# Row sums of a 67 MB array: blocks of 32 rows with a store each, a body on VectorE alone, and a two-piece last row

## The chip, the cores and the metric

The kernel runs on one core of a Trainium2 chip. The metric is the time of an execution on the device in microseconds (us), as a median of several executions. The granted clock was 1.00 in every profiled run.

A profiled "span" is about 1.8 us shorter than the timed execution, because it leaves out part of start and end.

## The reference

```python
def setup_inputs():
    batch, seq, dim = 32, 512, 1024
    return {"x": np.random.randn(batch, seq, dim).astype(np.float32)}

def reference(x):
    return np.sum(x, axis=-1).astype(np.float32)
```

There are 16384 rows of 1024 floats, 67.1 MB in, and 64 KB out. Each of the 128 partitions sums 128 rows.

## The kernel before

A partition owns 128 consecutive rows, so neighbouring partitions lie 128 x 4 KB = 512 KB apart in HBM. A full tile holds 16 rows a partition (8.39 MB). Three buffers rotate. VectorE sums one half of the tile in one instruction and ScalarE the other half row by row. The last tile is loaded in falling sizes, so that little is left to add when the last bytes arrive.

```python
    x_p = x_flat.rearrange("(p c) d -> p (c d)", p=P)      # C = 128 rows a partition
    out2d = out.rearrange("a (b c) -> (a b) c", c=C)
    G = 16
    T = C // G
    xpool = ctx.enter_context(tc.tile_pool(name="x", bufs=3))
    res = rpool.tile([P, C], F32, name="res")
    ...
    for t in range(T - 1):
        c0 = t * G
        xt = xpool.tile([P, G * D], F32, tag="xt", name="xt")
        load(xt, c0, 0, G * D)
        rows_dve(xt, c0, 0, G // 2)            # one tensor_reduce over 8 rows
        rows_act(xt, c0, G // 2, G // 2)       # 8 activations with accum_out

    c0 = (T - 1) * G                           # the last tile: 8, 4, 2, 1 rows, then
    ...                                        # the last row in 512 + 256 + 256 columns
    for j, n in runs:
        if n > 1:
            rows_dve(xt, c0, j, n // 2)
            rows_act(xt, c0, j + n // 2, n // 2)
        else:
            rows_act(xt, c0, j, 1)
    acc = [part[:, 0:1], part[:, 1:2], res[:, C - 1 : C]]
    for i, (a, b) in enumerate(zip(cuts, cuts[1:])):
        pairs_dve(xt, a, b, acc[i - 1] if i else 0.0, acc[i])   # half + half, summed

    nc.sync.dma_start(out=out2d, in_=res)      # 512 B a partition
```

Of the kernel before, what the change touches and what calls it, by code (L numbers as in the profile page):

```python
# [1 line left out]

# [4 lines left out]

F32 = mybir.dt.float32
ADD = mybir.AluOpType.add


@with_exitstack
def kernel(
    ctx: ExitStack,
    tc: tile.TileContext,
    x: bass.AP,
    out: bass.AP,
):
    nc = tc.nc
    P = nc.NUM_PARTITIONS  # L20

    x_flat = x.flatten_outer_dims()
    R, D = x_flat.shape
    assert R % P == 0
    C = R // P

    x_p = x_flat.rearrange("(p c) d -> p (c d)", p=P)
    out2d = out.rearrange("a (b c) -> (a b) c", c=C)

    G = 16  # L30
    assert C % G == 0
    T = C // G

    xpool = ctx.enter_context(tc.tile_pool(name="x", bufs=3))
    rpool = ctx.enter_context(tc.tile_pool(name="res", bufs=1))
    res = rpool.tile([P, C], F32, name="res")
    part = rpool.tile([P, 4], F32, name="part")

    def load(xt, c0, a, b):
        nc.sync.dma_start(out=xt[:, a:b], in_=x_p[:, c0 * D + a : c0 * D + b])  # L40

    def rows_dve(xt, c0, j, n):
        nc.vector.tensor_reduce(  # L43
            out=res[:, c0 + j : c0 + j + n],
            in_=xt[:, j * D : (j + n) * D].rearrange("p (j d) -> p j d", d=D),
            axis=mybir.AxisListType.X,
            op=ADD,
        )

    def rows_act(xt, c0, j, n):  # L50
        for i in range(j, j + n):
            v = xt[:, i * D : (i + 1) * D]
            nc.scalar.activation(  # L53
                out=v,
                in_=v,
                func=mybir.ActivationFunctionType.Copy,
                accum_out=res[:, c0 + i : c0 + i + 1],
            )

    def pairs_dve(xt, a, b, first, acc):  # L60
        h = (b - a) // 2
        nc.vector.tensor_tensor_reduce(  # L62
            out=xt[:, a : a + h],
            in0=xt[:, a : a + h],
            in1=xt[:, a + h : b],
            scale=1.0,
            scalar=first,
            op0=ADD,
            op1=ADD,
            accum_out=acc,  # L70
        )

    for t in range(T - 1):
        c0 = t * G
        xt = xpool.tile([P, G * D], F32, tag="xt", name="xt")
        load(xt, c0, 0, G * D)
        rows_dve(xt, c0, 0, G // 2)
        rows_act(xt, c0, G // 2, G // 2)

    c0 = (T - 1) * G  # L80
    xt = xpool.tile([P, G * D], F32, tag="xt", name="xt")
    j = 0
    runs = []
    for n in (8, 4, 2, 1):
        load(xt, c0, j * D, (j + n) * D)
        runs.append((j, n))
        j += n
    cuts = [j * D + k for k in (0, D // 2, 3 * D // 4, D)]
    for a, b in zip(cuts, cuts[1:]):
        load(xt, c0, a, b)  # L90

    for j, n in runs:
        if n > 1:
            rows_dve(xt, c0, j, n // 2)
            rows_act(xt, c0, j + n // 2, n // 2)
        else:
            rows_act(xt, c0, j, 1)
    acc = [part[:, 0:1], part[:, 1:2], res[:, C - 1 : C]]
    for i, (a, b) in enumerate(zip(cuts, cuts[1:])):
        pairs_dve(xt, a, b, acc[i - 1] if i else 0.0, acc[i])  # L100

    nc.sync.dma_start(out=out2d, in_=res)


# [1 line left out]
_INS = ['x']  # L106
_OUTS = [((32, 512), 'float32')]


# [23 lines left out]
```

## Time and profile before

| | before |
|---|---|
| median of 3 runs | 163.96 us (163.91 to 163.97) |
| span of the profiled run (164.13 us) | 162.4 us |
| DMA engines busy (page, part 3) | 96.3% |
| VectorE, ScalarE busy (page, part 1) | 43%, 43% |
| interval of full tiles | 19.4 us for 8.39 MB |
| last load landed; last VectorE instruction ended | 159.12; 159.86 us |

The first lines are from the page of the kernel before: busy time of the engines, the DMA queues with the share of time in which the 16 DMA engines were busy, and the shares of the chain that ended last.

```profile
DVE 69.9 (43%) x16; ACT 69.0 (43%) x129; POOL 0.2 (0%) x4
...
q1 hardware_dynamic: 2160, 67.18, 96.3%
...
DMA 85%; DVE 11%; SPq 1%; issue 1%; DVEq 0%
```

Next is the timeline of VectorE in the kernel before. The columns are start, duration (both us), engine, line, operation and shapes. The bracket gives the idle time before the instruction and what ended it. CUSTOM_DVE_ANT_0 is the instruction that adds two halves and sums the result (`pairs_dve`); DVE_READ_ACCUMULATOR2_ANT then writes its sum out.

```profile
22.97 8.69 DVE L43 TENSOR_REDUCE res<-xt 128x8 f32<-128x8192 f32 x1 [22.97 <-DMA xt<-in_x_dram]
42.27 8.69 DVE L43 TENSOR_REDUCE res<-xt 128x8 f32<-128x8192 f32 x1 [10.62 <-DMA xt<-in_x_dram]
61.96 8.69 DVE L43 TENSOR_REDUCE res<-xt 128x8 f32<-128x8192 f32 x1 [11.00 <-DMA xt<-in_x_dram]
...
139.44 8.69 DVE L43 TENSOR_REDUCE res<-xt 128x8 f32<-128x8192 f32 x1 [10.66 <-DMA xt<-in_x_dram]
149.16 4.42 DVE L43 TENSOR_REDUCE res<-xt 128x4 f32<-128x4096 f32 x1 [1.04 <-DMA xt<-in_x_dram]
...
158.64 0.42 DVE L62 CUSTOM_DVE_ANT_0 xt<-xt 128x256 f32<-128x256 f32 x1 [0.87 <-DMA xt<-in_x_dram]
158.99 0.08 DVE L62 DVE_READ_ACCUMULATOR2_ANT part<- 128x1 f32 x1
159.11 0.35 DVE L62 CUSTOM_DVE_ANT_0 xt<-xt,part 128x128 f32<-128x128 f32 x1
159.38 0.08 DVE L62 DVE_READ_ACCUMULATOR2_ANT part<- 128x1 f32 x1
159.50 0.35 DVE L62 CUSTOM_DVE_ANT_0 xt<-xt,part 128x128 f32<-128x128 f32 x1
159.78 0.08 DVE L62 DVE_READ_ACCUMULATOR2_ANT res<- 128x1 f32 x1
```

VectorE waits for a load before every full tile, so the load stream sets the pace. Tiles come 19.3 to 19.7 us apart, about 432 GB/s. The Trainium skill, "DMA: Bandwidth & Descriptors" (Specifications), puts the fabric ceiling at 435 GB/s, and this trace agrees. So in a kernel like this the time is made of three parts: when the stream gets going, 67.1 MB at a fixed rate, and what follows the last byte.

The first tile is there only at 22.97 us, although its load was issued at 0.73 us and a tile takes 19.4.

### The profile page before, as it was taken

To read this page: it belongs to the slowest core of one execution; us is meant where nothing else is said; L and a number is where in the kernel's file an instruction comes from. 1 tells how busy PE (TensorE), PEld (TensorE's weight loads), DVE (VectorE), ACT (ScalarE), POOL (GpSimd) and SP (SyncE) were. 2 spreads that over 40 slices of the span, in tenths; PEclk is the share of its full clock that TensorE was granted. 3 is DMA by queue.
4 is the path that set the end of the run, shared out by engine and by line. 5 is a ranking of instruction groups with operands and counts; after the bars stand their busy time and mean duration, and the time that the engine had idled before them with its cause. 6 is when DMAs were issued, how large, how long until landed. Compare 5 with 4: busy or idle time off the path is not lost.

```text
span 162.4 us, 220 instructions
## 1 busy us (share of the span) xinstructions
DVE 69.9 (43%) x16; ACT 69.0 (43%) x129; POOL 0.2 (0%) x4
## 2 busy tenths in 40 slices
DVE  0000039700595007940099101990049700697882
ACT  3000039700594007930099101990039600696881
POOL 0000000000000000000000000000000000000000
DMA  7979989989989989989997997997997997999980
GB/s 258 517 323 452 517 355 420 517 371 404 501 355 436 517 371 404 517 371 404 517 452 325 517 468 307 517 468 323 501 484 323 484 484 307 452 420 408 418 350 20
DMA packets 2161, 67.18 MB, mean 414 GB/s; under 512 B 240, under 2 KB 624, under 8 KB 880
## 3 DMA queue, kind: packets, MB, share of 16 engines
q1 hardware_dynamic: 2160, 67.18, 96.3%
q14 instruction: 1, 0.01, 0.0%
HBM read 67.11 MB, written 0.07 MB: 414 GB/s over the span
## 4 chain that ended last, share of the span: by engine, by line
DMA 85%; DVE 11%; SPq 1%; issue 1%; DVEq 0%
DMA xt<-in_x_dram 85%; DVE res L43 11%; SPq L40 1%; DVE xt L62 0%; DVE part L62 0%; DVEq L62 0%; DVEq L128 0%
## 5 line engine op out<-in xcount | busy, mean ns | idle before, releaser
L43 DVE TENSOR_REDUCE res<-xt 128x8 f32<-128x8192 f32 (+3 forms) x10 | 68.7, 6873 | 89.0 <-DMA xt<-in_x_dram 89.0
L53 ACT ACTIVATE xt<-xt 128x1024 f32<-128x1024 f32 x64 | 66.7, 1043 | 89.3 <-DMA xt<-in_x_dram 89.1
L53 ACT ACTIVATION_READ_ACCUMULATOR xt<-xt 128x1 f32 x64 | 11.9, 187 | 0.0
L53 ACT ACT_TABLE_LOAD x1 | 1.3, 1283 | 0.7 <-PEq L117 0.7
L62 DVE CUSTOM_DVE_ANT_0 xt<-xt 128x256 f32<-128x256 f32 x1 | 0.4, 425 | 0.9 <-DMA xt<-in_x_dram 0.9
L62 DVE CUSTOM_DVE_ANT_0 xt<-xt,part 128x128 f32<-128x128 f32 x2 | 0.7, 352 | 0.1
L62 DVE DVE_READ_ACCUMULATOR2_ANT part<- 128x1 f32 x2 | 0.2, 82 | 0.0
L117 POOL MEMSET const-bfloat16-1.0<- 128x1 bf16 x1 | 0.1, 101 | 0.0
L117 POOL MEMSET const-uint8-127<- 128x1 uint8 x1 | 0.1, 101 | 0.0
L117 POOL MEMSET const-float32-0.0<- 128x1 f32 x1 | 0.1, 98 | 0.2 <-issue 0.2
L117 POOL MEMSET const-float32-1.0<- 128x1 f32 x1 | 0.1, 98 | 0.0
L62 DVE DVE_READ_ACCUMULATOR2_ANT res<- 128x1 f32 x1 | 0.1, 84 | 0.0
## 6 DMA issues: line engine op xcount, KB each, us to landing
xt<-in_x_dram SPq DMA_DIRECT2D x1, 4096.0 KB, 39.7
xt<-in_x_dram SPq DMA_DIRECT2D x1, 2048.0 KB, 44.2
xt<-in_x_dram SPq DMA_DIRECT2D x1, 1024.0 KB, 46.2
xt<-in_x_dram SPq DMA_DIRECT2D x1, 512.0 KB, 47.0
xt<-in_x_dram SPq DMA_DIRECT2D x1, 256.0 KB, 47.1
xt<-in_x_dram SPq DMA_DIRECT2D x2, 128.0 KB, 43.0
xt<-in_x_dram SPq DMA_DIRECT2D x7, 49.4
out_dram<-res SPq DMA_DIRECT2D x1, 64.0 KB, 1.5
```

The source lines that it names most:

```text
L40: nc.sync.dma_start(out=xt[:, a:b], in_=x_p[:, c0 * D + a : c0 * D + b])
L43: nc.vector.tensor_reduce(out=res[:, c0 + j : c0 + j + n], in_=xt[:, j * D : (j + n) * D].rearrange("p (j d) -> p j d", d=D), axis=mybir.A ...
L53: nc.scalar.activation(out=v, in_=v, func=mybir.ActivationFunctionType.Copy, accum_out=res[:, c0 + i : c0 + i + 1],)
L62: nc.vector.tensor_tensor_reduce(out=xt[:, a : a + h], in0=xt[:, a : a + h], in1=xt[:, a + h : b], scale=1.0, scalar=first, op0=ADD, op1=A ...
L117: nc = _bacc.Bacc("TRN2", target_bir_lowering=False, num_devices=1)
```

## The change

The intent is to shorten what follows the last byte. The rows are split into four blocks of 4096. Within a block a partition owns 32 consecutive rows, so partitions lie 32 x 4 KB = 128 KB apart. Each block has its own result tile and its own store; three of the four stores go out during the stream, and the last one has 128 B a partition instead of 512 B. VectorE alone sums the body, so that ScalarE is free. ScalarE joins for 6 rows of the last full tile and for the tail. The last row comes in two pieces (640 and 384 columns) instead of three. The first piece is shared by both engines, and a last reduce adds 384 columns and the two partial sums.

The diff is shortened: `...` marks what is left out, and long calls stand on one line.

```diff
+BLOCKS = (32, 32, 32, 32)
...
+ACT_ROWS = 6
+CUT = 640
...
+    def block(r0, n):
+        x_b = x_flat[r0 : r0 + P * n].rearrange("(p c) d -> p (c d)", p=P)
+        out_b = out_flat[r0 : r0 + P * n].rearrange("(p c) -> p c", p=P)
+        return x_b, out_b, rpool.tile([P, n], F32, name=f"res{r0}")
...
-    for t in range(T - 1):
...
-        load(xt, c0, 0, G * D)
-        rows_dve(xt, c0, 0, G // 2)
-        rows_act(xt, c0, G // 2, G // 2)
...
+    for b, n in enumerate(BLOCKS):
+        x_b, out_b, res = block(r0, n)
...
+            nc.sync.dma_start(out=xt[:, 0 : m * D], in_=x_b[:, c * D : (c + m) * D])
+            a = ACT_ROWS if final and c + m == whole else 0
+            rows_dve(xt, res, 0, m - a, c)
+            rows_act(xt, res, m - a, a, c + m - a)
+            c += m
+        if not final:
+            nc.scalar.dma_start(out=out_b, in_=res)
...
-    for i, (a, b) in enumerate(zip(cuts, cuts[1:])):
-        pairs_dve(xt, a, b, acc[i - 1] if i else 0.0, acc[i])
-    nc.sync.dma_start(out=out2d, in_=res)
+    row_pairs_dve(xt, res, i + 2, c + i + 2)          # the last row but one
+    nc.vector.tensor_reduce(out=tail[:, D : D + 1], in_=tail[:, 0 : CUT // 2], axis=X, op=ADD)
+    sum_act(tail[:, CUT // 2 : CUT], tail[:, D + 1 : D + 2])
+    nc.vector.tensor_reduce(out=res[:, n - 1 : n], in_=tail[:, CUT : D + 2], axis=X, op=ADD)
+    nc.sync.dma_start(out=out_b, in_=res)
```

More of the change, by code (lines that the diff above doesn't have):

```diff
@@ L9 @@
 ADD = mybir.AluOpType.add
+COPY = mybir.ActivationFunctionType.Copy
+X = mybir.AxisListType.X
+BLOCKS = (32, 32, 32, 32)
+G = 16
+ACT_ROWS = 6
+CUT = 640
 @with_exitstack
@@ L23 @@
     R, D = x_flat.shape
-    assert R % P == 0
     C = R // P
-    x_p = x_flat.rearrange("(p c) d -> p (c d)", p=P)
-    out2d = out.rearrange("a (b c) -> (a b) c", c=C)
-    G = 16
-    assert C % G == 0
-    T = C // G
+    assert R % P == 0 and sum(BLOCKS) == C
+    out_flat = out.rearrange("a (b c) -> (a b c)", c=1)
     xpool = ctx.enter_context(tc.tile_pool(name="x", bufs=3))
     rpool = ctx.enter_context(tc.tile_pool(name="res", bufs=1))
-    res = rpool.tile([P, C], F32, name="res")
@@ L37, with rows_dve @@
-    part = rpool.tile([P, 4], F32, name="part")
-    def load(xt, c0, a, b):
-        nc.sync.dma_start(out=xt[:, a:b], in_=x_p[:, c0 * D + a : c0 * D + b])
-    def rows_dve(xt, c0, j, n):
+    tail = rpool.tile([P, D + 2], F32, name="tail")
+    def rows_dve(xt, res, j, n, c):
         nc.vector.tensor_reduce(
-            out=res[:, c0 + j : c0 + j + n],
+            out=res[:, c : c + n],
             in_=xt[:, j * D : (j + n) * D].rearrange("p (j d) -> p j d", d=D),
-            axis=mybir.AxisListType.X,
+            axis=X,
@@ L47, in rows_dve @@
             op=ADD,
         )
-    def rows_act(xt, c0, j, n):
-        for i in range(j, j + n):
-            v = xt[:, i * D : (i + 1) * D]
-            nc.scalar.activation(
-                out=v,
-                in_=v,
-                func=mybir.ActivationFunctionType.Copy,
-                accum_out=res[:, c0 + i : c0 + i + 1],
-            )
-    def pairs_dve(xt, a, b, first, acc):
-        h = (b - a) // 2
-        nc.vector.tensor_tensor_reduce(
-            out=xt[:, a : a + h],
-            in0=xt[:, a : a + h],
-            in1=xt[:, a + h : b],
-            scale=1.0,
-            scalar=first,
-            op0=ADD,
-            op1=ADD,
-            accum_out=acc,
-        )
@@ L73 @@
-    for t in range(T - 1):
-        c0 = t * G
-        xt = xpool.tile([P, G * D], F32, tag="xt", name="xt")
-        load(xt, c0, 0, G * D)
-        rows_dve(xt, c0, 0, G // 2)
-        rows_act(xt, c0, G // 2, G // 2)
-    c0 = (T - 1) * G
-    xt = xpool.tile([P, G * D], F32, tag="xt", name="xt")
-    j = 0
-    runs = []
-    for n in (8, 4, 2, 1):
-        load(xt, c0, j * D, (j + n) * D)
-        runs.append((j, n))
-        j += n
-    cuts = [j * D + k for k in (0, D // 2, 3 * D // 4, D)]
@@ L89, with sum_act @@
-    for a, b in zip(cuts, cuts[1:]):
-        load(xt, c0, a, b)
-    for j, n in runs:
-        if n > 1:
-            rows_dve(xt, c0, j, n // 2)
-            rows_act(xt, c0, j + n // 2, n // 2)
-        else:
-            rows_act(xt, c0, j, 1)
-    acc = [part[:, 0:1], part[:, 1:2], res[:, C - 1 : C]]
-    for i, (a, b) in enumerate(zip(cuts, cuts[1:])):
-        pairs_dve(xt, a, b, acc[i - 1] if i else 0.0, acc[i])
-    nc.sync.dma_start(out=out2d, in_=res)
+    def sum_act(v, acc):
+        nc.scalar.activation(out=v, in_=v, func=COPY, accum_out=acc)
@@ new lines, in rows_act, with row_pairs_dve @@
+    def rows_act(xt, res, j, n, c):
+        for i in range(n):
+            sum_act(xt[:, (j + i) * D : (j + i + 1) * D], res[:, c + i : c + i + 1])
+    def row_pairs_dve(xt, res, j, c):
+        h = D // 2
+        a, b = xt[:, j * D : j * D + h], xt[:, j * D + h : (j + 1) * D]
+        nc.vector.tensor_tensor_reduce(
+            out=a, in0=a, in1=b, scale=1.0, scalar=0.0, op0=ADD, op1=ADD,
+            accum_out=res[:, c : c + 1],
+        )
+    def block(r0, n):
+        x_b = x_flat[r0 : r0 + P * n].rearrange("(p c) d -> p (c d)", p=P)
+        out_b = out_flat[r0 : r0 + P * n].rearrange("(p c) -> p c", p=P)
+        return x_b, out_b, rpool.tile([P, n], F32, name=f"res{r0}")
@@ new lines @@
+    r0 = 0
+    for b, n in enumerate(BLOCKS):
+        x_b, out_b, res = block(r0, n)
+        r0 += P * n
+        final = b == len(BLOCKS) - 1
+        whole = n - G - (n % G if final and n % G else 0) if final else n
+        c = 0
+        while c < whole:
+            m = min(G, whole - c)
+            xt = xpool.tile([P, G * D], F32, tag="xt", name="xt")
+            nc.sync.dma_start(out=xt[:, 0 : m * D], in_=x_b[:, c * D : (c + m) * D])
[5 more added lines that the diff above has]
+            nc.scalar.dma_start(out=out_b, in_=res)
@@ new lines @@
+    xt = xpool.tile([P, G * D], F32, tag="xt", name="xt")
+    first = n - c - 8
+    cuts = [0, first, first + 4, first + 6, first + 7]
+    for i, k in zip(cuts, cuts[1:]):
+        nc.sync.dma_start(out=xt[:, i * D : k * D], in_=x_b[:, (c + i) * D : (c + k) * D])
+    last = (n - 1) * D
+    nc.sync.dma_start(out=tail[:, 0:CUT], in_=x_b[:, last : last + CUT])
+    nc.sync.dma_start(out=tail[:, CUT:D], in_=x_b[:, last + CUT : last + D])
+    for i, k in zip(cuts[:2], cuts[1:3]):
+        h = (k - i + 1) // 2
+        rows_dve(xt, res, i, h, c + i)
+        rows_act(xt, res, i + h, k - i - h, c + i + h)
@@ L106 @@
+    i = cuts[2]
+    rows_dve(xt, res, i, 1, c + i)
+    rows_act(xt, res, i + 1, 1, c + i + 1)
+    row_pairs_dve(xt, res, i + 2, c + i + 2)
+    nc.vector.tensor_reduce(
+        out=tail[:, D : D + 1], in_=tail[:, 0 : CUT // 2], axis=X, op=ADD
+    )
+    sum_act(tail[:, CUT // 2 : CUT], tail[:, D + 1 : D + 2])
+    nc.vector.tensor_reduce(
+        out=res[:, n - 1 : n], in_=tail[:, CUT : D + 2], axis=X, op=ADD
+    )
+    nc.sync.dma_start(out=out_b, in_=res)
 _INS = ['x']
```

## The prediction

> **What bounds the kernel now.** The DMA engines: busy 96.3% of the 162.4 us span on the page; VectorE and ScalarE 43% each. The chain of waits gives DMA 85%, VectorE 11%. In the timeline the reduces of full tiles start at 42.27, 61.96, 81.33, 100.73, 120.09 and 139.44 us: 19.4 us per 8.39 MB tile, about 432 GB/s. The Trainium skill ("DMA: Bandwidth & Descriptors", Specifications) puts the fabric ceiling at 435 GB/s; this trace agrees, so the body has nothing to gain. A 64 KB packet takes 2.42 us. Only about 2 us of start and the tail remain: the last load lands near 159.1 us, VectorE ends at 159.86, the store lands about 1.5 us after issue.
>
> **What the change does.**
> 1. Body: VectorE alone sums 16 rows. From the groups by form, 8 rows take 8.69 us and 4 take 4.42: 1.067 us a row and 0.15 fixed, so 17.2 us a tile (estimate), below the 19.4 us arrival. Tiles come free 8.5 us later, still about 11 us before DMA would starve. Gain 0, loss 0.
> 2. Row blocks: the distance between partitions in HBM falls from 512 KB to 128 KB; packets stay 64 KB. The engines run at their own rate, so I expect nothing; it is the least certain term.
> 3. Three early stores of 16 KB on ScalarE's queue. The skill (same page, "Issuing engines are not separate DMA queues") says they interleave on the same 16 engines. Here a 512 B store packet took 27 ns, and one foreign 8 KB packet delayed its engine by about 0.3 us, its own transfer time. Eight small packets per engine and store: about 0.15 us a store (estimate), +0.2 to +0.5 us in all, on the critical path. ScalarE's fewer instructions may save one instruction fetch (0.3 us on one engine).
> 4. Final store: 128 B instead of 512 B a partition: 0 to -0.15 us.
> 5. ScalarE's table load (1.28 us) moves behind the third store, at about 137.5 us, before its rows arrive at 139.4: harmless.
> 6. Tail: VectorE takes 10 rows of the last full tile (10.8 us, estimate) instead of 8 (8.69). It ends near 150.3, after the next piece has landed (149.1), and keeps a backlog: 4 rows to 154.7, 2 rows to 157.0, 1 row to 158.2, the row by pairs to 159.0, 320 columns to 159.5, the last 386 to 160.1. Before: 159.86. Two pieces instead of three gain nothing while this backlog lasts: +0.25 us.
>
> **Sum.** 163.96 + 0.3 (stores) + 0.25 (tail) - 0.1 (small store) - 0.1 (fetch) = 164.3 us; 8 in 10: 163.5 to 165.2. Faster by over 2%: 0.02; within 2%: 0.95; slower by over 2%: 0.03.
>
> **What would show it.** Step 1: full-tile reduces of 17.2 us starting 19.4 us apart, each idle about 2 us on the DMA. Step 2: 64 KB packets still 2.42 us. Step 3: tiles after a store arriving 0.1 to 0.2 us late. Step 5: the first ScalarE row waits for DMA, not for the table. Step 6: the tail's reduces follow one another without idle time, and the last ends over 0.5 us after the last landing. If VectorE idles before the last two reduces, step 6 is wrong and the change gains up to 0.4 us.
>
> **What would make it wrong.** Small stores that stall the load stream at each switch between queues (+1 to +5 us); a memory layout in which 128 KB spacing (or, now, 512 KB) makes the partitions collide (a few us either way); a table load that waits behind 64 KB packets.

## The result

The changed kernel took 163.40 us (median of 4 runs, 163.23 to 163.75), beside 163.97 us (163.91 to 164.00) for the kernel before. Ratios here are the mean time of one kernel's fast runs over the mean of the other's in the same rounds, so they are not quite the ratio of the medians. The ratio is 0.9968, with a 95% interval of 0.9951 to 0.9986. That is no change at the 2% mark, but it is a real gain of about half a microsecond where 0.3 us of loss had been predicted. The measured time lies 0.1 us below the stated range.

The same lines of the page, for the changed kernel (q1 is the queue of the loads and the last store, q10 that of the three early stores):

```profile
DVE 123.5 (76%) x14; ACT 15.8 (10%) x29; POOL 0.2 (0%) x4
...
q1 hardware_dynamic: 2016, 67.13, 96.6%
q10 hardware_dynamic: 432, 0.05, 0.2%
...
DMA 76%; DVE 22%; ACT 0%; issue 0%; ACTq 0%
```

And the timeline of VectorE:

```profile
22.68 17.22 DVE L40 TENSOR_REDUCE res<-xt 128x16 f32<-128x16384 f32 x1 [22.68 <-DMA xt<-in_x_dram]
42.04 17.22 DVE L40 TENSOR_REDUCE res<-xt 128x16 f32<-128x16384 f32 x1 [2.14 <-DMA xt<-in_x_dram]
...
139.34 18.46 DVE L40 TENSOR_REDUCE res<-xt 128x10 f32<-128x10240 f32 x4 [2.11 <-DMA xt<-in_x_dram]
157.86 0.69 DVE L57 CUSTOM_DVE_ANT_0 xt<-xt 128x512 f32<-128x512 f32 x1
158.48 0.08 DVE L57 DVE_READ_ACCUMULATOR2_ANT res<- 128x1 f32 x1
158.58 0.49 DVE L102 TENSOR_REDUCE tail<-tail 128x1 f32<-128x320 f32 x1
159.17 0.55 DVE L106 TENSOR_REDUCE res<-tail 128x1 f32<-128x386 f32 x1
```

The body went as foreseen: a reduce of 16 rows takes 17.22 us (estimated 17.2), and VectorE still waits over 2 us for each tile. The chain's larger share of VectorE (22% against 11%) means nothing here. A buffer now comes free later, so the chain passes through a reduce, but the loads do not wait for it: the packets of the 16 DMA engines follow one another with less than 0.1 us of gap between 6 and 157 us.

Two things stand out. The first tile is there 0.29 us sooner, although up to there only the loads' addresses have changed, and ScalarE's table load, which ran at 0.72 us in the kernel before, has moved to the end. And the tail, in which the prediction saw a growing backlog, ends 0.71 us after the last landing (159.73 against 159.01). Before it was 0.75 us.

What my theory then was: the gain is the layout's and the small final store's; the tail and the body are neutral. The rivals were that the new tail brings the gain, as intended; that taking ScalarE's work out of the body does; and that the early stores do.

### The profile page after: what moved, and what is told of

It is laid out like the page before. It is cut to its first block, busy times and chain, and to the rows that moved or that the text cites. A ratio compares the mean times of both kernels' runs of the same rounds, so it can differ in the third digit from the quotient of the medians.

```text
span 162.0 us, 116 instructions
## 1 busy us (share of the span) xinstructions
DVE 123.5 (76%) x14; ACT 15.8 (10%) x29; POOL 0.2 (0%) x4
## 4 chain that ended last, share of the span: by engine, by line
DMA 76%; DVE 22%; ACT 0%; issue 0%; ACTq 0%
DMA xt<-in_x_dram 39%; DMA tail<-in_x_dram 22%; DVE res L40 21%; DMA out_dram<-res 15%; DVE res L106 0%; ACT tail L48 0%; ACTq L135 0%
## 5 line engine op out<-in xcount | busy, mean ns | idle before, releaser
L40 DVE TENSOR_REDUCE res<-xt 128x16 f32<-128x16384 f32 (+4 forms) x10 | 121.8, 12203 | 36.0 <-DMA xt<-in_x_dram 36.0
L48 ACT ACT_TABLE_LOAD x1 | 1.3, 1283 | 137.7 <-DVE res L40 137.7
L48 ACT ACTIVATE xt<-xt 128x1024 f32<-128x1024 f32 x13 | 13.6, 1045 | 4.7 <-DMA xt<-in_x_dram 4.7
L48 ACT ACTIVATION_READ_ACCUMULATOR xt<-xt 128x1 f32 x13 | 2.4, 186 | 0.0
L57 DVE CUSTOM_DVE_ANT_0 xt<-xt 128x512 f32<-128x512 f32 x1 | 0.7, 693 | 0.1
L106 DVE TENSOR_REDUCE res<-tail 128x1 f32<-128x386 f32 x1 | 0.6, 554 | 0.1
L48 ACT ACTIVATE tail<-tail 128x320 f32<-128x320 f32 x1 | 0.5, 469 | 1.0 <-DMA tail<-in_x_dram 1.0
L102 DVE TENSOR_REDUCE tail<-tail 128x1 f32<-128x320 f32 x1 | 0.5, 486 | 0.0
```

Source lines behind the costliest of these rows:

```text
L40: nc.vector.tensor_reduce(out=res[:, c : c + n], in_=xt[:, j * D : (j + n) * D].rearrange("p (j d) -> p j d", d=D), axis=X, op=ADD,)
L48: nc.scalar.activation(out=v, in_=v, func=COPY, accum_out=acc)
L57: nc.vector.tensor_tensor_reduce(out=a, in0=a, in1=b, scale=1.0, scalar=0.0, op0=ADD, op1=ADD, accum_out=res[:, c : c + 1],)
L102: nc.vector.tensor_reduce(out=tail[:, D : D + 1], in_=tail[:, 0 : CUT // 2], axis=X, op=ADD)
L106: nc.vector.tensor_reduce(out=res[:, n - 1 : n], in_=tail[:, CUT : D + 2], axis=X, op=ADD)
```

## The experiments

Twelve experiments were run. R1 and E1 to E3 share 11 runs of the kernel before (median 164.10 us). E4 to E7, on the same chip six minutes later, were compared with these same 11 runs and one more (164.09), so they had hardly any run of the kernel before beside them. E8 to E11 ran on another chip, with 11 runs of the kernel before of their own (163.99).

### R1: the changed kernel once more

No edit.

> The changed kernel once more, for a second trace and for the spread of its times (163.23 to 163.75 us in four runs; the profiled run was the slowest of them). In the profiled run 64 KB packets took 2.45 to 2.50 us between 38 and 78 us of the span, against 2.42 elsewhere, and two tiles there came 0.2 and 0.4 us late. If that is a passing disturbance, this trace lacks it and the run takes 163.2 to 163.4 us; if it belongs to the second row block or to the first store, it is there again at the same place.

Measured: 163.35 us (163.12 to 163.65), ratio 0.9955 (0.9941 to 0.9968). The profiled run was among its fastest, at 163.12 us. This is its VectorE timeline, with the first two full tiles and the two around the second store:

```profile
22.53 17.22 DVE L40 TENSOR_REDUCE res<-xt 128x16 f32<-128x16384 f32 x1 [22.53 <-DMA xt<-in_x_dram]
41.88 17.22 DVE L40 TENSOR_REDUCE res<-xt 128x16 f32<-128x16384 f32 x1 [2.12 <-DMA xt<-in_x_dram]
...
99.96 17.22 DVE L40 TENSOR_REDUCE res<-xt 128x16 f32<-128x16384 f32 x1 [2.09 <-DMA xt<-in_x_dram]
119.37 17.22 DVE L40 TENSOR_REDUCE res<-xt 128x16 f32<-128x16384 f32 x1 [2.19 <-DMA xt<-in_x_dram]
138.70 10.82 DVE L40 TENSOR_REDUCE res<-xt 128x10 f32<-128x10240 f32 x1 [2.11 <-DMA xt<-in_x_dram]
```

The slow stretch of the first trace (38 to 78 us, packets of 2.45 to 2.50 us) is absent, so it is a passing disturbance. Later traces show such stretches too, at other places and in kernels of both layouts (E1, E3, E4, E5, E8, E10), and the trace of the kernel before has a short stall (packets of up to 2.89 us at 41 to 42 us; the tile then came 19.69 us after the one ahead of it). In three kernels the profiled run that has a long one was the slowest of its kernel's runs (163.75 us for the first trace, 163.89 for E3, 163.74 for E10); in E1 and E4 it was in the middle. They are likely to make much of the scatter between runs, but the other runs have no traces to show it. What causes them is open.

### E1: the blocks undone

```diff
-BLOCKS = (32, 32, 32, 32)
+BLOCKS = (128,)
```

> Undoes the row blocks alone: one block of 128 rows a partition, so no early stores, a final store of 512 B a partition, and 512 KB between partitions as in the kernel before; VectorE's body and the new tail stay. If the gain of 0.55 us is the tail's, 163.5 us stays, plus about 0.1 us for the larger final store: 163.5 to 163.6. If it is the layout's or the small final store's, it goes back to 163.8 to 164.0, and the landings of a tile spread over 1.1 to 1.2 us from the first engine to the last as before (0.45 us in the changed kernel).

Measured: 164.03 us (163.67 to 164.32), ratio to before 0.9993 (0.9978 to 1.0008). The gain is gone, although the new tail and VectorE's body are still there. The expected spread came only in part: the landings of a tile lay 0.7 to 0.8 us apart. So the spread is not a safe mark, but the first tile is again late, at 22.98 us.

### E2: blocks and stores, but the old distance

```diff
-        x_b = x_flat[r0 : r0 + P * n].rearrange("(p c) d -> p (c d)", p=P)
-        out_b = out_flat[r0 : r0 + P * n].rearrange("(p c) -> p c", p=P)
+        k = r0 // P
+        x_b = x_flat.rearrange("(p c) d -> p (c d)", p=P)[:, k * D : (k + n) * D]
+        out_b = out_flat.rearrange("(p c) -> p c", p=P)[:, k : k + n]
```

> Keeps four blocks, three early stores and the small final store, but takes each block as 32 columns of the old layout, so that partitions lie 512 KB apart in HBM as before. If the 128 KB distance is what brings the engines closer together (spread of a tile's landings 0.45 us against 1.2), the spread returns to about 1.2 us and the time rises by 0.2 to 0.4 us, to 163.6 to 163.8. If the distance does not matter: 163.4 and a spread of 0.45.

Measured: 163.62 us (163.57 to 163.66), ratio 0.9972 (0.9960 to 0.9984). That is 0.27 us slower than R1 by the medians, though the two intervals against the kernel before overlap. The store count and sizes are R1's; what differs is the distance of the input's pieces, and with it that of the results (512 B apart instead of side by side). The spread was 0.7 to 0.9 us, again between the two values named. Its first reduce starts at 23.11 us:

```profile
23.11 17.22 DVE L40 TENSOR_REDUCE res<-xt 128x16 f32<-128x16384 f32 x1 [23.11 <-DMA xt<-in_x_dram]
```

E2 is still 0.48 us faster than the kernel before, at the old distance, so the distance is not the whole gain. Part of the rest is in the trace: from the end of the last VectorE instruction to the end of the span it is 2.25 us in E2 and R1, 2.49 us in the kernel before and 2.51 us in E4. About 0.13 us of this is the quicker landing of the smaller store (step 4 below). The other 0.1 us comes after that landing. SyncE, which issues the loads and the final store, closes the program with a row of semaphore waits. In E2, R1, E11 and the changed kernel the wait for the final store is the last of them, and the span ends 0.79 us after the landing. Where one more wait follows it is 0.88 us (before, E5, E8, E9, E10), with two 0.92 to 0.94 (E1, E3, E4, E6), with three 0.99 (E7). The prediction doesn't speak of this order; that it came out well in the changed kernel is luck.

### E3: no early stores (wrong result)

```diff
-        if not final:
-            nc.scalar.dma_start(out=out_b, in_=res)
```

> The changed kernel without its three early stores; three quarters of the result is not written, so the result is wrong on purpose. It measures what the stores cost on the critical path. The prediction said 0.2 to 0.5 us: then 162.9 to 163.2 us. If their 27 packets an engine cost only their own 13 ns each, 0.35 us or less: 163.05 to 163.4. If they cost nothing: 163.4.

Measured: 163.36 us (163.24 to 163.89), beside R1's 163.35. Three quarters of the output is unwritten, as intended. No cost of the early stores shows in the time, but E3 is not a clean removal: its closing waits take 0.15 us longer than R1's (0.94 against 0.79, see E2), which can hide a cost of that size. In R1's timeline the tiles that arrive while the first two stores are in flight come 19.42 and 19.41 us after the tile ahead of them, where its other tiles come after 19.31 to 19.35. So a store holds the stream up by about 0.07 us; E2 (19.44 and 19.42) and E8 (19.41) show the same. Its packets took 13 ns each.

### E4: the new tail alone

In the changed kernel's code, which makes it the kernel before with the new tail:

```diff
-BLOCKS = (32, 32, 32, 32)
+BLOCKS = (128,)
...
-            a = ACT_ROWS if final and c + m == whole else 0
+            a = ACT_ROWS if final and c + m == whole else m // 2
```

> The kernel before with the new tail alone (10 rows on VectorE and 6 on ScalarE in the last full tile, last row in two pieces); one block, one store, both engines in the body. The prediction's step 6 says 0.25 us slower than before. The traces say that reduces that follow one another overlap by 0.08 us each, so that VectorE keeps no backlog past the last landing, and ends 0.1 to 0.2 us sooner: 0.1 to 0.2 us faster than before, near the one-block kernel's 164.03.

Measured: 163.97 us (163.76 to 164.45), ratio 0.9999 (0.9984 to 1.0013). The new tail alone is worth nothing that can be told, neither the predicted loss of 0.25 us nor a gain of 0.2. In its trace the last reduce ends 0.72 us after the last landing (159.61 against 158.89). Its first and last full tiles:

```profile
23.21 8.69 DVE L40 TENSOR_REDUCE res<-xt 128x8 f32<-128x8192 f32 x1 [23.21 <-DMA xt<-in_x_dram]
...
139.28 18.46 DVE L40 TENSOR_REDUCE res<-xt 128x10 f32<-128x10240 f32 x4 [10.66 <-DMA xt<-in_x_dram]
```

### E5: VectorE's body alone

```diff
-        rows_dve(xt, c0, 0, G // 2)
-        rows_act(xt, c0, G // 2, G // 2)
+        n = G if t < T - 2 else G // 2
+        rows_dve(xt, c0, 0, n)
+        rows_act(xt, c0, n, G - n)
```

> The kernel before with VectorE alone in the first six tiles, nothing else changed. Body reduces of 17.2 us against arrivals of 19.4: no difference from before (within 0.1 us). If the body's split mattered (two engines in the buffers at once, or one instruction fetch), 0.1 to 0.3 us faster.

Measured: 163.95 us (163.79 to 164.53), ratio 0.9998 (0.9984 to 1.0012). No difference, as the prediction's step 1 said. The instruction fetch that the kernel before has at 87.56 us of its span is gone from this trace, and no gain from that shows in the time.

### E6: blocks and stores alone

The kernel before with its own body and tail; inputs, results and stores by blocks:

```diff
+    B = 32
+    x_bs = x_flat.rearrange("(k p c) d -> k p (c d)", p=P, c=B)
+    outs = out.rearrange("a (b c) -> (a b c)", c=1).rearrange("(k p c) -> k p c", p=P, c=B)
...
+    ress = [rpool.tile([P, B], F32, name=f"res{k}") for k in range(C // B)]
...
+        if (c0 + G) % B == 0:
+            nc.scalar.dma_start(out=outs[c0 // B], in_=ress[c0 // B])
```

> The kernel before with the four row blocks and their stores alone (128 KB between partitions, three early stores, small final store), old body and old tail. If the gain is the blocks', as undoing them said (163.35 against 164.03 us), this has most of it: 0.5 to 0.7 us faster than before, 163.4 to 163.6. The first tile then lands at 22.5 to 22.65 us of the span instead of 22.95 and a tile's landings spread over 0.45 to 0.65 us. If the gain needs the new tail too, it is under 0.3 us.

Measured: 163.73 us (4 runs, 163.54 to 163.94), ratio 0.9975 (0.9960 to 0.9989). This is the only one of the three parts that is faster alone, by 0.36 us of medians. That is less than the 0.5 to 0.7 us expected, and a tile's landings spread over 0.7 to 1.0 us, not 0.45 to 0.65. Its trace contains a stall of 0.3 us at 65.9 us. The packet records put it down to an instruction fetch (8 KB, 0.31 us, at 65.58 us): the next tile came 19.65 us after the one ahead of it, the others after 19.33 to 19.41. The fetch in the kernel before cost its tile about 0.04 us (19.40). So a fetch can cost its whole time in one run and next to nothing in another; the changed kernel's trace has none.

E6 also settles a rival, ScalarE's table load at the start. E6 has it, as the kernel before does, and its first tile is early; E1, E2 and E5 do not have it there, and theirs is late.

```profile
0.72 1.28 ACT L54 ACT_TABLE_LOAD   x1 [0.72 <-PEq L120]
...
22.73 8.69 DVE L44 TENSOR_REDUCE res<-xt 128x8 f32<-128x8192 f32 x1 [22.73 <-DMA xt<-in_x_dram]
```

### E7: 64 KB apart

```diff
-BLOCKS = (32, 32, 32, 32)
+BLOCKS = (16, 16, 16, 16, 16, 16, 32)
```

> The changed kernel with six blocks of 16 rows and one of 32: partitions lie 64 KB apart, each full tile is one contiguous 8 MB piece of the input, and there are six early stores instead of three. If a shorter distance between partitions is what makes the first packets shorter, the first tile lands at 22.5 us or sooner and the time is 163.1 to 163.4 us, 0.2 us of extra stores included (0.07 us each in the second trace). If only the old 512 KB distance is bad, the landing stays at 22.5 to 22.65 and the time rises by those stores: 163.4 to 163.6.

Measured: 163.61 us (4 runs, 163.39 to 163.95), ratio 0.9973 (0.9958 to 0.9988). A shorter distance than 128 KB brings nothing more: the first reduce starts at 22.72 us. Of its 0.26 us over R1, 0.2 us comes after the final store's landing (0.99 against 0.79 us, see E2).

### E8 to E10: where the distance matters, and which one

```diff
-BLOCKS = (32, 32, 32, 32)
+BLOCKS = (32, 96)        # E8: 128 KB for the first two tiles, then 384 KB
+BLOCKS = (64, 64)        # E9: 256 KB
+BLOCKS = (96, 32)        # E10: 384 KB for the first six tiles, then 128 KB
```

> The changed kernel with two blocks, 32 and 96 rows: only the first two tiles lie 128 KB apart, the other six 384 KB; one early store, final store of 384 B a partition. In nine traces the latest engine's first packet ended at 5.26 to 5.45 us where partitions lay 64 or 128 KB apart and at 5.67 to 5.81 where they lay 512 KB apart, and all later packets took the same. If that first wave is all that the distance does: first packets end by 5.45, first tile lands at 22.5 to 22.7, time 163.3 to 163.6 (the larger final store costs about 0.1, two early stores less save as much). If the distance in the rest of the stream matters: 163.7 to 164.0 although the first tile lands early.

> Two blocks of 64 rows: 256 KB apart. If the first wave's delay grows with the distance, the latest first packet ends between 5.45 and 5.67 us and the time lies between 163.4 and 164.0; if it comes only at 512 KB, 5.26 to 5.45 and 163.3 to 163.6 us.

> Two blocks of 96 and 32 rows: the first six tiles lie 384 KB apart, which is no power of two; the final store is 128 B as in the changed kernel. If powers of two collide, the first packets end by 5.45 us as at 128 KB and the time is 163.2 to 163.5; if it is the distance itself, they end near 5.6 us and the time is 163.5 to 163.8.

Measured: E8 163.32 us (163.21 to 163.52), ratio 0.9955 (0.9939 to 0.9970). E9 163.42 us (163.36 to 164.17), ratio 0.9969 (0.9951 to 0.9988). E10 163.32 us (163.18 to 163.74), ratio 0.9958 (0.9943 to 0.9974). (One wording of E8's expectation needs mending: it counts nine traces, but there were ten, five of each kind.)

All three are as fast as the changed kernel within the scatter. E10 says most: 384 KB is three times the changed kernel's distance and starts as early, at 22.59 us:

```profile
22.59 17.22 DVE L40 TENSOR_REDUCE res<-xt 128x16 f32<-128x16384 f32 x1 [22.59 <-DMA xt<-in_x_dram]
41.90 17.22 DVE L40 TENSOR_REDUCE res<-xt 128x16 f32<-128x16384 f32 x1 [2.10 <-DMA xt<-in_x_dram]
```

The next table sets all fourteen traces side by side by the distance of the first tile. "First packet" is when the last of the 16 DMA engines finished its first 64 KB packet, taken from the trace's packet records. "First tile" is when VectorE's first reduce started.

| distance | traces | first packet, us | first tile, us |
|---|---|---|---|
| 512 KB | before, E1, E2, E4, E5 | 5.67 to 5.81 | 22.97 to 23.21, mean 23.07 |
| 384 KB | E10 | 5.30 | 22.59 |
| 256 KB | E9 | 5.52 | 22.77 |
| 128 KB | after, R1, E3, E6, E8, E11 | 5.26 to 5.42 | 22.53 to 22.73, mean 22.65 |
| 64 KB | E7 | 5.45 | 22.72 |

The 512 KB traces and the others do not overlap. With 512 KB the slowest engine's first packet ends about 0.37 us later than with 128 KB, and the first tile comes 0.42 us later. The first packets do not take longer at 512 KB (2.90 to 3.08 us on average over the 16 engines, against 2.98 to 3.23 us elsewhere); they start later (at 2.13 to 2.40 us on average, against 1.83 to 2.05).

After that the stream is as fast at either distance. From the first full tile to the seventh it takes 116.17 us in R1 (22.53 to 138.70, 128 KB, two stores in between) and 116.07 us in E4 (23.21 to 139.28, 512 KB, no store); over all traces it is 116.07 to 116.47 us at 512 KB and 116.17 to 116.73 at 128 KB. An engine that is late with its first packet is late with all that follow, since its packets come without gaps (in the traces of before, R1, E2 and E4 all 16 engines have a packet under way from 6 to 157 us). So the distance acts once, at the start, and the end of the load stream inherits it, as far as slow stretches leave it to be seen: the last load landed at 159.02 us on average at 512 KB (158.89 to 159.18) and at 158.74 us at 128 KB (158.38 to 159.01).

### E11: a tail without a backlog

```diff
-ACT_ROWS = 6
+ACT_ROWS = 8
```

> The changed kernel with 8 rows of the last full tile on VectorE and 8 on ScalarE (10 and 6 in the change). The prediction said that VectorE's backlog from the 10 rows costs 0.25 us or more at the end: then 0.2 us faster, 163.1 to 163.2. In the trace the backlog is used up just as the last pieces land (VectorE free at 158.56, piece landed at 158.55): then the last reduce still ends 0.7 us after the last landing and the time stays at 163.35 within 0.1, with VectorE idle before each piece of the tail.

Measured: 163.23 us (163.10 to 163.46), ratio 0.9951 (0.9937 to 0.9965). That is within the scatter of R1 and E10. The timeline of VectorE in its tail shows idle time before each piece down to the last row but one (0.18 us there), so there is no backlog:

```profile
148.59 4.42 DVE L40 TENSOR_REDUCE res<-xt 128x4 f32<-128x4096 f32 x1 [1.05 <-DMA xt<-in_x_dram]
153.47 2.29 DVE L40 TENSOR_REDUCE res<-xt 128x2 f32<-128x2048 f32 x1 [0.46 <-DMA xt<-in_x_dram]
155.96 1.22 DVE L40 TENSOR_REDUCE res<-xt 128x1 f32<-128x1024 f32 x1 [0.21 <-DMA xt<-in_x_dram]
157.37 0.69 DVE L57 CUSTOM_DVE_ANT_0 xt<-xt 128x512 f32<-128x512 f32 x1 [0.18 <-DMA xt<-in_x_dram]
157.98 0.08 DVE L57 DVE_READ_ACCUMULATOR2_ANT res<- 128x1 f32 x1
158.11 0.48 DVE L102 TENSOR_REDUCE tail<-tail 128x1 f32<-128x320 f32 x1
158.70 0.56 DVE L106 TENSOR_REDUCE res<-tail 128x1 f32<-128x386 f32 x1
```

The last load landed at 158.51 us and the last reduce ended at 159.26, which is 0.75 us: no less than with the backlog (0.71 us in the changed kernel). In this tail ScalarE's half of the 640-column piece, not VectorE, is what the last reduce waits for. None of the kernels tried beats the changed one by more than the scatter.

## Why the prediction was wrong, point by point

- **What bounds the kernel: right.** The stream runs at its rate in all fourteen traces, and neither the body (E5) nor the tail (E4) moves the time.
- **Step 1, body: right.** 17.22 us a tile, 2 us of idle, no gain or loss (E5, ratio 0.9998).
- **Step 2, row blocks, "I expect nothing": this step failed.** It reasoned from the rate ("the engines run at their own rate"), and the rate is indeed the same. It left out that the start of the stream is also on the critical path. There 512 KB costs about 0.42 us at the first tile (23.07 against 22.65), and everything after inherits it. In time, E2 against R1 gives 0.27 us for the distance alone (anything from about 0 to 0.55 by the scatter of five runs each, so the first tile is the surer witness), and E6 gives 0.36 us for blocks with stores. The prediction did call it its least certain term, and did name 512 KB spacing as a possible culprit, but it gave the term zero and a range too narrow for it. The Trainium skill's page has a warning here ("DMA: Bandwidth & Descriptors", Latency and other measured facts, on HBM row pitch at large powers of two: in copies between HBM tensors, 207 GB/s at 512 KiB against a full 214). This case shows no such loss of rate, only the late first packets.
- **Step 3, early stores, +0.2 to +0.5 us: too large.** About 0.07 us for each of the first two in R1's tiles, so 0.15 to 0.2 us for three (an estimate), and nothing visible in the time, where E3's longer closing can hide as much. The 128 B packets took 13 ns; the estimate had started from the 27 ns of 512 B packets. The fetch saved, -0.1 us in the sum, shows no gain in E5.
- **Step 4, small final store, 0 to -0.15 us: right.** From the end of the last VectorE instruction to the landing of the store it was 1.57 to 1.61 us with 512 B a partition (before, E1, E4, E5) and 1.45 to 1.49 us with 128 B (after, R1, E2, E3, E6, E7, E10, E11): about 0.13 us less. The skill's page (Specifications) says that below 512 B the DMA engine does a read-modify-write; whether it did is not shown here. The 128 B packets were shorter than the 512 B ones (13 against 27 ns), though not in proportion. The step missed the 0.1 us of the closing waits (see E2), which came by luck.
- **Step 5, table load: right.** It ran at 137.7 us, was over in 1.28 us, and the rows' wait was for DMA.
- **Step 6, tail, +0.25 us: this step failed in size.** The backlog was there, and the reduces ran without idle time. But it was summed from single durations, and reduces that follow one another overlap. The groups by form of the changed kernel give 10.82, 4.41, 2.28 and 1.21 us, together 18.71, while the timeline has the four in 18.46 us: 0.08 us for each join. So VectorE was free at 158.56 us, just as the 640-column piece landed (158.55), and the last reduce ended 0.71 us after the last landing, 0.3 us sooner than predicted (160.1 against 159.1 us). Before it was 0.75 us. VectorE was even idle before the last two reduces, for 0.02 and 0.10 us, which the prediction had named as a sign against this step. The tail is neutral (E4, E11). The sign proposed for it, "the last ends over 0.5 us after the last landing", was true of both kernels and so told nothing.

The terms as measured: -0.42 (start), -0.13 (final store), -0.1 (closing waits), 0 (tail), 0 to +0.2 (stores), together -0.45 to -0.65 us. The gain of the changed kernel was 0.57 us by medians and 0.75 us beside R1. Up to 0.3 us is thus not assigned. As much is left over in E2: at the old distance these terms give 0.23 us at most, and it gained 0.48, each of its five runs below every run of the kernel before. Slow stretches, stalls and instruction fetches in the runs without a trace may make it up, but no run shows this, and it stays open. The change was meant to shorten what follows the last byte; its largest measured term lies at the start, where the prediction expected nothing.

The mechanism of the late first packets is open too. A delay that grows steadily with the distance is not what the traces show (384 KB starts earlier than 256), so collisions at large powers of two are a possible reading. But only 512 KB was clearly late and 256 KB lies at the edge; 256 and 384 KB have one trace each, on another chip than the 512 KB experiments. The first packets start later rather than take longer. And the distance also sets how far a tile reaches over the input (64 MB at 512 KB, 48 MB at 384 KB), which no run separates from it.

## What to carry to other kernels

When a kernel already streams at the DMA rate, look at the first load as well as at the last: in this kernel a layout that changed no packet size and no rate was worth about 0.4 us at the first tile, because the DMA engines finished their first packets sooner. When adding up back-to-back instructions, take the sum from a run of them in a timeline rather than from single durations, and before shortening a tail, check how long after the last landing it ends. An effect of a few tenths of a per cent needs several rounds and more than one trace of each kernel; two traces of the changed kernel here differ by 0.6 us (spans of 162.0 and 161.3 us).

## What the Trainium skill lacked or had wrong

- "DMA: Bandwidth & Descriptors" (HBM row pitch at large powers of two) speaks of the rate alone. Here loads with partitions 512 KB apart streamed as fast as at 128 KB (116.07 to 116.47 against 116.17 to 116.73 us for six tiles), but the slowest engine's first packet ended at 5.67 to 5.81 us instead of 5.26 to 5.45 us at 64 and 128 KB.
- The same page has no figure for the first 64 KB packet of a stream, nor for a steady one. Here the first took 2.9 to 3.2 us on average over the 16 engines, and later ones 2.42 us.
- The same page warns of stores under 512 B (read-modify-write). Here a store of 128 x 128 B landed about 0.13 us sooner than one of 128 x 512 B, and its packets took 13 ns each against 27 ns: longer for each byte, but not for each store.
- "VectorE: DVE Perf Modes" (Terms, DRAIN) says that the next instruction can't issue until the pipe is empty. In the records here, reduces that follow one another overlap by 0.08 us (18.46 us for a sum of 18.71), so the row reads stricter than they do; the page's own section on the drain already allows an earlier start for some instructions.
- No page read speaks of the passing stretches in which 64 KB packets take 2.45 to 2.7 us on most engines; in the trace of E3 they added about 0.8 us to an engine's packets on average (55 packets of 2.433 us, against 2.419 in R1).
